# A hybrid encoder layer: the second FFN matrix loaded once, kept on chip and mixed in place, with another order of the products

## The chip, the cores and the metric

The kernel runs on one core of a Trainium2 chip. The metric is the device time of the program in microseconds. The profile shows one execution of it. TensorE (PE) multiplies matrices, and its loads of the stationary operand have a row of their own (PEld). VectorE (DVE), ScalarE (ACT) and GpSimd (POOL) work element by element. SyncE (SP) issues transfers (DMA) from its queue, in order.

## The reference, cut to what matters

The layer computes, for 1024 tokens of width 1024: modulated RMS norm, a combined projection, two attention mixers, a gated merge and an output projection with a residual, and then a gated feed-forward network (FFN) with a residual. The change lies in the last line of it, the second FFN matrix of 2816 x 1024:

```python
h2 = rms_norm(x, g_norm2[l]) * (1.0 + sc2) + sh2
a, up = jnp.split(h2 @ w_ffn_in[l], 2, axis=-1)
x = x + gt2 * ((jax.nn.silu(a) * up) @ w_ffn_out[l])
```

## The kernel before, in words

**Precision.** Every operand of a large product is split in two, a high half `whi` (a copy by ACT, line 118) and a low half `wlo` (a subtraction on DVE or POOL, line 119). A block product is then three matmuls: high x high, high x low, low x high (`PASS`). `wload` fetches a block of 128 x 512 into one of six small `raw` tiles on the SP queue. `wsplit` makes its halves in ten `whi` and ten `wlo` tiles. As a step takes two of each, at most five steps of the inner loop are on chip as halves at a time.

**The second FFN matrix.** The gated activations (1024 x 2816) and the matrix (2816 x 1024) are cut into 2 x 2 blocks, and their product is formed with seven block products instead of eight (Strassen's scheme in Winograd's form). The combinations of the activations were formed in the stage before and lie in DRAM as `ga_d[g, k]`, transposed, seven of them with eleven tiles of 128 x 512 each. The matrix enters the first three products as plain blocks B11, B21, B22, and the last four as differences:

- T1 = B12 - B11, T3 = B22 - B12, T2 = B22 - T1, T4 = B21 - T2.

`PRODS` gives for each product the combination of the activations and the block of the matrix. In the order of the kernel before the products are P1, P2, P3, P6, P5, P7, P4. `prod2(n)` forms one of them: for each of the eleven steps k it calls `operands` (load and split both sides) and then issues 12 matmuls into four PSUM banks, 132 in all. The last product issues its last three steps together, bank by bank (`LASTK`). Consecutive products use two sets of four banks in turn.

**Where the matrix comes from.** In the first three products `operands` loads a plain block through a raw tile (`wload(w2blk(...))`). Besides, during the second and third products, `w2_mix(k)` loads all four blocks of row k again into 44 resident tiles of the pool `w2m` (88 KB per partition), and forms the four differences in place on DVE (lines 1477 to 1480). The last four products read them from there. Low halves of the resident tiles are made by POOL for k < 10 in the fourth to sixth product and k < 5 in the seventh, all others by DVE.

**Memory.** The pool `f2`, which holds `gt2`, the outputs `c11` to `c22` and the `x2` tiles, takes the place of `h2T`, the operand of the first FFN matrix. `gt2` is the first tile in it and lies where the first half of `h2T` lay, so its load (line 1465) waits for the last matmul that reads it. The pool `w2m` takes the place of the pools of the first FFN matrix, from the end where `t3` and `t2` lay, which the last column product no longer reads.

**The outputs.** After each product DVE adds its banks into the blocks `c11`, `c12`, `c21`, `c22` that need it (ACT copies the first). `finish` then scales a finished block by `gt2` (DVE, line 1522), adds the residual `x2` loaded from DRAM (POOL, line 1523) and stores it. The last block, `c21`, is scaled and gets its residual ahead of the last product. P4 is then scaled and added bank by bank (lines 1557, 1558) and stored.

**What sets the order.** TensorE's order is the written one throughout (`manual_schedule`). In this last stage the order on ACT, DVE, POOL and SP is set by the framework's planner, which places instructions in the order in which they become ready in its own simulated time. `pin` (`keep_in_program_order`) ties an instruction behind the one that was written just before it for the same engine. It is an order of issue and not a wait for completion. The loads of the resident tiles are pinned.

Of the kernel before, what the change touches and what calls it, by code (L numbers as in the profile page):

```python
# [10 lines left out]
F32 = mybir.dt.float32  # L11
# [9 lines left out]
HT = 11  # L21
# [22 lines left out]
def hybrid_layer(ctx: ExitStack, tc: tile.TileContext, x, colp, wada1, wada2, bada2, wqkv, wg, wpa, wpb,  # L44
                 wo, w1, w2, hgain, ropeg, rope, rbias, bmask, g2r, out):
    nc = tc.nc

    def pool(name, side, **kw):
        return tc.alloc_tile_pool(name=name, bufs=1, side=side, reuse_waits="tile", **kw)
# [25 lines left out]
    def bank(tag):  # L75
        return ps.tile([128, 512], F32, tag=tag, name="ps_" + tag)
# [29 lines left out]
    def fview(ap):  # L106
        return ap.bitcast(F32)

    def wload(src, n):
        raw = wp.tile([128, 512], F32, tag="raw", bufs=NRAW, name="raw")  # L110
        nc.sync.dma_start(raw[:, :n], src)
        return raw[:, :n]

    def wsplit(r, eng=None):
        n = r.shape[1]
        hi = wp.tile([128, 512], F32R, tag="hi", bufs=NHL, name="whi")
        lo = wp.tile([128, 512], F32R, tag="lo", bufs=NHL, name="wlo")
        nc.scalar.activation(hi[:, :n], r, AF.Copy)  # L118
        (eng or nc.gpsimd).tensor_sub(lo[:, :n], r, fview(hi[:, :n]))  # L119
        return hi, lo  # L120
# [404 lines left out]
    class Cluster:  # L525
# [5 lines left out]
        def add(self, I):  # L531
            I.c0 = self.keys
            self.items.append(I)
            self.keys += I.nkb * 128
# [204 lines left out]
    pin = tc.keep_in_program_order  # L739
# [726 lines left out]
    def w2blk(r, c, k):  # L1466
        return w2[(k + HT * r) * 128:(k + HT * r + 1) * 128, c * 512:c * 512 + 512]

    w2p = pool("w2m", "right")
    w2m = {}  # L1470

    def w2_mix(k):
        b = [w2p.tile([128, 512], F32, name=f"m{n}_{k}") for n in range(4)]
        for z, (r, c) in zip(b, ((0, 0), (0, 1), (1, 1), (1, 0))):
            pin(nc.sync.dma_start(z, w2blk(r, c, k)))
        t1, t3, t2, t4 = b
        nc.vector.tensor_sub(t1, t3, t1)  # L1477
        nc.vector.tensor_sub(t3, t2, t3)  # L1478
        nc.vector.tensor_sub(t2, t2, t1)  # L1479
        nc.vector.tensor_sub(t4, t4, t2)  # L1480
        w2m[k] = t1, t2, t3, t4

    PRODS = ((0, (0, 0)), (1, (1, 0)), (6, (1, 1)), (4, 1), (3, 0), (5, 2), (2, 3))
    LASTK = 3

    def operands(n, k):
        g, m = PRODS[n]
        a = wload(ga_d[g, k], 512)
        b = w2m[k][m] if n > 2 else wload(w2blk(*m, k), 512)
        return wsplit(a, nc.vector), wsplit(b, nc.vector if n < 3 or k == HT - 1 or (n == 6 and k > 4) else None)  # L1490

    def blocks(name):
        return [fp.tile([128, 512], F32, name=f"{name}{m}") for m in range(4)]

    def prod2(n):
        pb = [bank(("ds", "vt")[n % 2][m // 2]) for m in range(4)]
        last = LASTK if n == 6 else 0

        def mm(k, m, o):
            for i, (a, b) in enumerate(PASS):  # L1500
                nc.tensor.matmul(pb[m], o[0][a][:, m * 128:(m + 1) * 128], o[1][b],  # L1501
                                 start=(k == 0 and i == 0), stop=(k == HT - 1 and i == 2))

        for k in range(HT - last):
            o = operands(n, k)
            if n in (1, 2) and k % 2 == n - 1:
                w2_mix((k + (n - 1) * HT) // 2)
            for m in range(4):
                mm(k, m, o)
        ops = {k: operands(n, k) for k in range(HT - last, HT)}  # L1510
        for m in range(4):
            for k in ops:
                mm(k, m, ops[k])
        return pb

    def finish(rh, c, z, last=None):
        cs = slice(c * 512, c * 512 + 512)
        for m in range(4):
            t = rh * 4 + m
            xt = fp.tile([128, 512], F32, tag="x2", bufs=4, name="x2")  # L1520
            nc.sync.dma_start(xt, x2_d[t * 128:(t + 1) * 128, cs])
            nc.vector.tensor_mul(z[m], z[m], gt2[:, cs])  # L1522
            nc.gpsimd.tensor_add(z[m], z[m], xt)
            if last is None:
                nc.sync.dma_start(out[t * 128:(t + 1) * 128, cs], z[m])

    c11, c12, c21, c22 = (blocks(z) for z in ("c11", "c12", "c21", "c22"))
    add = nc.vector.tensor_add
    p1 = prod2(0)
    for m in range(4):  # L1530
        nc.scalar.activation(c21[m], p1[m], AF.Copy)
    p2 = prod2(1)
    for m in range(4):
        add(c11[m], c21[m], p2[m])  # L1534
    p3 = prod2(2)
    for m in range(4):
        add(c12[m], c21[m], p3[m])
    p6 = prod2(3)
    for m in range(4):
        add(c21[m], c21[m], p6[m])  # L1540
        add(c12[m], c12[m], p6[m])
    finish(0, 0, c11)
    p5 = prod2(4)
    for m in range(4):
        add(c22[m], c21[m], p5[m])
        add(c12[m], c12[m], p5[m])
    finish(0, 1, c12)
    p7 = prod2(5)
    for m in range(4):
        add(c21[m], c21[m], p7[m])  # L1550
        add(c22[m], c22[m], p7[m])
    finish(1, 1, c22)
    finish(1, 0, c21, True)
    p4 = prod2(6)
# [111 lines left out]
```

## Time and profile before

| | |
|---|---|
| median of the runs | 1508.73 us (1504.3 to 1509.01, three runs) |
| profiled execution, its own time | 1513.95 us |
| its span, first to last instruction | 1512.1 us, 24226 instructions |
| mean granted TensorE clock | 0.998 |
| last stage (line 1501), starts of the first and last matmul | 1295.3 and 1507.1 us |
| second FFN matrix, resident tiles | 44 loads of 256 KB (line 1475) |

All durations in the prediction are of the profiled execution; its own time stands above the median of the runs. In a timeline a row has the start, the duration, the engine with its line and operation, the tile written and the tiles read, and in brackets the idle time before it and what ended it. The duration of a DVE instruction overlaps that of the next a little, so the pitch between two starts is the smaller number. `SPq` rows are issues of transfers, not their landing.

### The profile page before, as it was taken

The page shows a single profiled execution, that of the slowest core. Times are in us where ns is not written, and L with a number is a line of the kernel's source. Part 1 is how long each engine was busy: PE and PEld are TensorE (multiplying, and loading weights), DVE is VectorE, ACT ScalarE, POOL GpSimd, SP SyncE. Part 2 cuts the span into 40 slices and gives each one's busy share as a digit, 9 for nine tenths or more (in the row PEclk, how much of TensorE's full clock was granted, in tenths as well). Part 3 has the DMA queues.
Part 4 walks back from the last instruction along what each step waited for, and adds up shares of the span by engine and source line. Part 5 has one row for each costly group of instructions (what it writes and reads, how often), then busy time and mean ns, then how long its engine had stood idle before and what let it go on. Part 6 is the DMA issues. An engine that isn't in the chain of part 4 may idle for free. (4 is left out here: it accounts for less than half of the span.)

```text
span 1512.1 us, 24226 instructions
## 1 busy us (share of the span) xinstructions
PE 1488.8 (98%) x8156; PEld 1267.5 (84%) x8156; DVE 1063.0 (70%) x2201; ACT 697.0 (46%) x1755; POOL 537.0 (36%) x540
## 2 busy tenths in 40 slices
PE   8999999999999999999999999999999999999998
PEld 7998989998888877788878888888888888887886
DVE  6877777766778724366565497788867777599468
ACT  5555665565766665245532344332222333354442
POOL 0332332321100040002361311677777776104464
PEclk9999999999999999999999999999999999999999
DMA  9625455645145164823553235345443334798342
GB/s 353 247 75 172 140 159 162 196 137 166 53 134 167 48 194 142 325 87 115 175 172 148 82 102 181 115 137 174 154 138 106 105 106 146 263 384 281 100 151 101
DMA packets 150636, 241.64 MB, mean 160 GB/s; under 512 B 26464, under 2 KB 69088, under 8 KB 149744
## 3 DMA queue, kind: packets, MB, share of 16 engines
q1 hardware_dynamic: 131936, 226.45, 45.6%
q10 hardware_dynamic: 18576, 13.64, 2.8%
q8 instruction: 65, 1.06, 0.3%
q14 instruction: 59, 0.48, 0.1%
HBM read 179.89 MB, written 60.15 MB: 159 GB/s over the span
## 5 line engine op out<-in xcount | busy, mean ns | idle before, releaser
L119 POOL TENSOR_TENSOR wlo<-raw,whi 128x512 fp32r<-128x512 f32 (+2 forms) x133 | 175.3, 1331 | 462.9 <-ACT whi L118 395.5
L118 ACT ACTIVATE whi<-raw 128x512 fp32r<-128x512 f32 (+1 forms) x348 | 203.1, 598 | 250.9 <-PE ps_t L1501 35.4
L312 PE MATMUL ps_d<-whi,hT 128*128 128x384 f32 x1152 | 311.1, 341 | 0.0
L119 DVE TENSOR_TENSOR wlo<-raw,whi 128x512 fp32r<-128x512 f32 (+1 forms) x215 | 184.3, 870 | 81.2 <-ACT whi L118 76.3
L312 PEld LDWEIGHTS ps_d<-whi,hT 128*128 128x128 f32 x1152 | 210.3, 189 | 5.2 <-ACT vs L350 2.6
L312 PE MATMUL ps_d<-wlo,hT 128*128 128x384 f32 x576 | 193.8, 336 | 1.8 <-DVE wlo L119 1.7
L312 PEld LDWEIGHTS ps_d<-wlo,hT 128*128 128x128 f32 x576 | 108.9, 189 | 2.8 <-DVE wlo L119 2.3
L118 ACT ACTIVATE whi<-ws 128x512 fp32r<-128x512 f32 x65 | 40.8, 628 | 127.3 <-DVE ws L1348 86.3
L1281 POOL TENSOR_TENSOR e<-e,c 128x512 f32<-128x512 f32 x44 | 69.0, 1569 | 60.5 <-DVE c L1411 36.4
L342 POOL TENSOR_TENSOR ra<-qn,rtab 128x64 f32<-128x64 f32 x48 | 16.3, 339 | 156.0 <-DVE qn L335 106.1
L119 POOL TENSOR_TENSOR wlo<-m,whi 128x512 fp32r<-128x512 f32 x35 | 51.4, 1478 | 54.7 <-ACT whi L118 54.7
L1279 ACT ACTIVATE e<-e 128x512 f32<-128x512 f32 x44 | 27.5, 630 | 91.4 <-DVE e L1414 64.0
L555 ACT ACTIVATE P<-P,st 128x256 f32<-128x256 f32 (+2 forms) x100 | 45.7, 458 | 39.7 <-DVE st L553 39.6
L712 PE MATMUL ps_d<-hT,whi 128*128 128x512 f32 x192 | 60.6, 397 | 0.0
L1331 PE MATMUL ps_v<-h2T,whi 128*128 128x512 f32 x192 | 59.2, 390 | 0.0
L1331 PE MATMUL ps_s<-h2T,whi 128*128 128x512 f32 x192 | 59.1, 389 | 0.0
L1331 PE MATMUL ps_d<-h2T,whi 128*128 128x512 f32 x184 | 56.8, 390 | 0.0
L129 ACT ACTIVATE ry<-ss,eps 128x4 f32<-128x4 f32 (+1 forms) x88 | 26.2, 298 | 64.7 <-DVE ss L333 47.8
L119 DVE TENSOR_TENSOR wlo<-ws,whi 128x512 fp32r<-128x512 f32 x45 | 49.7, 1106 | 8.5 <-ACT whi L118 8.5
L1280 DVE TENSOR_TENSOR e<-e 128x512 f32<-128x512 f32 x44 | 42.6, 975 | 16.6 <-ACT e L1279 16.5
L301 DVE SCALAR_TENSOR_TENSOR acc<-wa,cact,acc 128x512 f32<-128x512 f32 x56 | 42.0, 749 | 16.7 <-DMA wa<-in_wada_dram 16.5
L491 ACT ACTIVATE P<-P,sx 128x384 f32<-128x384 f32 (+1 forms) x64 | 37.1, 580 | 35.9 <-DVE sx L490 35.9
(445 smaller groups left out, 3965.6 us busy)
## 6 DMA issues: line engine op xcount, KB each, us to landing
raw<-in_w_dram SPq DMA_DIRECT2D x139, 256.0 KB
ga_d<-e SPq DMA_DIRECT2D x77, 256.0 KB
raw<-ga_d SPq DMA_DIRECT2D x77, 256.0 KB
wa<-in_wada_dram SPq DMA_DIRECT2D x32, 512.0 KB
raw<-in_wqkv_dram SPq DMA_DIRECT2D x80, 192.0 KB
m<-in_w_dram SPq DMA_DIRECT2D x44, 256.0 KB
raw<-in_wg_dram SPq DMA_DIRECT2D x42, 256.0 KB
xt<-in_x_dram SPq DMA_DIRECT2D x16, 512.0 KB
```

Of the source, the lines that this page charges most:

```text
L118: nc.scalar.activation(hi[:, :n], r, AF.Copy)
L119: (eng or nc.gpsimd).tensor_sub(lo[:, :n], r, fview(hi[:, :n]))
L129: nc.scalar.activation(y, ss, AF.Ln, scale=1.0 / n, bias=eps)
L301: nc.vector.scalar_tensor_tensor(ada_acc[c], wa, cact[:, kk:kk + 1], ada_acc[c], op0=ALU.mult, op1=ALU.add)
L312: nc.tensor.matmul(pd[:, :384], tok(a, k, t), U.w[k][b][:, :384], start=(k == 0 and i == 0), stop=(k == KT - 1 and i == 2))
L491: nc.scalar.activation(P[:nq, :nk], P[:nq, :nk], AF.Exp, scale=-1.0, bias=nm, accum_out=sm)
L555: nc.scalar.activation(C.P[h][:nq, c], C.P[h][:nq, c], AF.Exp, scale=-1.0, bias=nm, accum_out=sm)
L712: nc.tensor.matmul(st["p"], gw[i, br][j][a][:, kk * 128:(kk + 1) * 128], hT[b][:, k, hs], start=(k == 0 and q == 0), stop=(k == 7 and q == 2))
L1279: nc.scalar.activation(sg, a, AF.Sigmoid)
L1280: nc.vector.tensor_mul(sg, sg, a)
L1281: nc.gpsimd.tensor_mul(sg, sg, up)
L1331: nc.tensor.matmul(pb, w[p][:, k * 128:(k + 1) * 128], b[q][:, k], start=(k == 0 and i == 0), stop=(k == 3 and i == 2))
```

## The change

The resident tiles are loaded once and serve all seven products. `w2_load(s)` is called three steps ahead (`LOOK`). It loads the block that the product reads: B11 in the first, B21 together with B12 in the second, and B22 in the third, 44 loads in all, each pinned. The first three are written ahead of the first product, right behind the load of `gt2`. `operands` takes the matrix from these tiles in every product, so only the activations still go through the raw tiles.

`w2_mix(n, k)` forms one difference per step, in place: T1 in the third product, T3 in the fourth, T2 in the fifth, T4 in the sixth. Each is read one product later. For this the products run as P1, P2, P3, P5, P7, P6, P4. P6 is now added into three outputs after the sixth product, which makes four additions more, and `c12` is finished there, together with `c22` and `c21`, and no longer after the fifth. Low halves of the matrix are now made by DVE, except for k < 5 of the seventh product, which stay on POOL.

```diff
--- before.py
+++ after.py
@@ -1467,27 +1467,34 @@
         return w2[(k + HT * r) * 128:(k + HT * r + 1) * 128, c * 512:c * 512 + 512]
 
     w2p = pool("w2m", "right")
-    w2m = {}
-
-    def w2_mix(k):
-        b = [w2p.tile([128, 512], F32, name=f"m{n}_{k}") for n in range(4)]
-        for z, (r, c) in zip(b, ((0, 0), (0, 1), (1, 1), (1, 0))):
-            pin(nc.sync.dma_start(z, w2blk(r, c, k)))
-        t1, t3, t2, t4 = b
-        nc.vector.tensor_sub(t1, t3, t1)
-        nc.vector.tensor_sub(t3, t2, t3)
-        nc.vector.tensor_sub(t2, t2, t1)
-        nc.vector.tensor_sub(t4, t4, t2)
-        w2m[k] = t1, t2, t3, t4
-
-    PRODS = ((0, (0, 0)), (1, (1, 0)), (6, (1, 1)), (4, 1), (3, 0), (5, 2), (2, 3))
-    LASTK = 3
+    w2t = {}
+    PRODS = ((0, (0, 0)), (1, (1, 0)), (6, (1, 1)), (3, (0, 0)), (5, (0, 1)), (4, (1, 1)), (2, (1, 0)))
+    LASTK, LOOK = 3, 3
+
+    def w2_load(s):
+
+        n, k = divmod(s, HT)
+        if n < 3:
+            for b in (PRODS[n][1],) + (((0, 1),) if n == 1 else ()):
+                w2t[b, k] = w2p.tile([128, 512], F32, name=f"m{b[0]}{b[1]}_{k}")
+                pin(nc.sync.dma_start(w2t[b, k], w2blk(*b, k)))
+
+    def w2_mix(n, k):
+
+        t1, t3, t2, t4 = (w2t.get((b, k)) for b in ((0, 0), (0, 1), (1, 1), (1, 0)))
+        if n == 2:
+            nc.vector.tensor_sub(t1, t3, t1)
+        elif n == 3:
+            nc.vector.tensor_sub(t3, t2, t3)
+        elif n == 4:
+            nc.vector.tensor_sub(t2, t2, t1)
+        elif n == 5:
+            nc.vector.tensor_sub(t4, t4, t2)
 
     def operands(n, k):
-        g, m = PRODS[n]
+        g, b = PRODS[n]
         a = wload(ga_d[g, k], 512)
-        b = w2m[k][m] if n > 2 else wload(w2blk(*m, k), 512)
-        return wsplit(a, nc.vector), wsplit(b, nc.vector if n < 3 or k == HT - 1 or (n == 6 and k > 4) else None)
+        return wsplit(a, nc.vector), wsplit(w2t[b, k], None if n == 6 and k < 5 else nc.vector)
 
     def blocks(name):
         return [fp.tile([128, 512], F32, name=f"{name}{m}") for m in range(4)]
@@ -1502,9 +1509,9 @@
                                  start=(k == 0 and i == 0), stop=(k == HT - 1 and i == 2))
 
         for k in range(HT - last):
+            w2_load(n * HT + k + LOOK)
             o = operands(n, k)
-            if n in (1, 2) and k % 2 == n - 1:
-                w2_mix((k + (n - 1) * HT) // 2)
+            w2_mix(n, k)
             for m in range(4):
                 mm(k, m, o)
         ops = {k: operands(n, k) for k in range(HT - last, HT)}
@@ -1526,6 +1533,8 @@
 
     c11, c12, c21, c22 = (blocks(z) for z in ("c11", "c12", "c21", "c22"))
     add = nc.vector.tensor_add
+    for k in range(LOOK):
+        w2_load(k)
     p1 = prod2(0)
     for m in range(4):
         nc.scalar.activation(c21[m], p1[m], AF.Copy)
@@ -1535,20 +1544,21 @@
     p3 = prod2(2)
     for m in range(4):
         add(c12[m], c21[m], p3[m])
-    p6 = prod2(3)
-    for m in range(4):
-        add(c21[m], c21[m], p6[m])
-        add(c12[m], c12[m], p6[m])
     finish(0, 0, c11)
-    p5 = prod2(4)
+    p5 = prod2(3)
     for m in range(4):
         add(c22[m], c21[m], p5[m])
         add(c12[m], c12[m], p5[m])
-    finish(0, 1, c12)
-    p7 = prod2(5)
+    p7 = prod2(4)
     for m in range(4):
         add(c21[m], c21[m], p7[m])
         add(c22[m], c22[m], p7[m])
+    p6 = prod2(5)
+    for m in range(4):
+        add(c12[m], c12[m], p6[m])
+        add(c22[m], c22[m], p6[m])
+        add(c21[m], c21[m], p6[m])
+    finish(0, 1, c12)
     finish(1, 1, c22)
     finish(1, 0, c21, True)
     p4 = prod2(6)
```

## The prediction

> **What bounds the kernel now.** I read the page's busy shares first, then the last stage (the second FFN matrix, seven products of 132 matmuls) cut into its seven products, and then the timelines of the engines at the places where the change acts. The columns of the second fence are the stretch and its length, and then busy time and instructions of PE, PEld, DVE, ACT and POOL, the granted clock, the DMA share and GB/s.
>
> ```profile
> PE 1488.8 (98%) x8156; PEld 1267.5 (84%) x8156; DVE 1063.0 (70%) x2201; ACT 697.0 (46%) x1755; POOL 537.0 (36%) x540
> ```
>
> ```profile
> 1295.30:1325.20 29.90, 29.90 (x133) 24.79 (x132) 18.18 (x27) 12.26 (x21) 5.56 (x4) 1.00 0.96 325
> 1325.20:1355.20 30.00, 30.00 (x134) 24.83 (x134) 29.10 (x48) 16.44 (x28) 0.00 (x0) 1.00 1.04 385
> 1355.20:1387.00 31.80, 31.15 (x134) 24.52 (x133) 30.81 (x44) 12.22 (x21) 8.67 (x6) 1.00 0.98 341
> 1387.00:1417.00 30.00, 30.00 (x134) 24.87 (x133) 16.21 (x20) 13.48 (x25) 19.00 (x13) 1.00 0.45 122
> 1417.00:1446.90 29.90, 29.90 (x134) 24.77 (x133) 13.91 (x21) 12.68 (x23) 13.20 (x10) 1.00 0.32 99
> 1446.90:1476.80 29.90, 29.90 (x134) 24.76 (x133) 23.82 (x25) 12.68 (x23) 21.47 (x14) 1.00 0.51 168
> 1476.80:1507.70 30.90, 30.49 (x133) 24.26 (x131) 28.09 (x34) 7.94 (x14) 14.35 (x9) 1.00 0.29 100
> ```
>
> TensorE sets the time. A product costs it 29.9 us when nothing is late, which is 11 steps k of 2.72 us. Only the third (31.8, so 1.9 lost, of which I count 1.8 because its ends are rounded) and the seventh (30.9, 1.0 lost) are longer. So this stage has 2.8 us to give, and no edit in it can gain more than that. Every new wait of TensorE, however, is paid in full. The third product is the one where DVE (30.81 of 31.80) and the DMA engines (0.98) are both full. In the seventh DVE is full until the last operands are split:
>
> ```profile
> 1480.00:1490.00 10.00, 10.00 (x12) 1.00 0.48 161
> 1490.00:1500.00 10.00, 10.00 (x11) 1.00 0.20 75
> ```
>
> ```profile
> 1500.02 0.40 PE L1501 MATMUL ps_d<-whi 128*128 128x512 f32 x1
> 1500.66 0.51 PE L1501 MATMUL ps_d<-wlo,whi 128*128 128x512 f32 x1 [0.24 <-DVE wlo L119]
> ```
>
> Here TensorE stands for the last low half. DVE has no slack left in the seventh product, and this decides most of what follows.
>
> **The start of the stage.** In the kernel before, the blocks of the second matrix for the first three products go through the small raw tiles and were fetched during the first FFN matrix. In the changed kernel they go to the resident tiles, and each of these loads is pinned, that is, it stands on the SP queue behind the SP instruction that was written just before it. For the very first one that is the load of `gt2` (line 1465). The pin holds in the kernel before: the first resident load there left SP directly behind the raw load that is written ahead of it.
>
> ```profile
> 1312.24 0.36 SPq L111 DMA_DIRECT2D raw<-in_w_dram  x1
> 1312.64 1.47 SPq L1475 DMA_DIRECT2D m<-in_w_dram  x2
> ```
>
> `gt2` lies where the first half of `h2T` lay, so its load waits for the last matmul of the first FFN matrix, the one at 1295.09:
>
> ```profile
> 1295.09 0.39 PE L1331 MATMUL ps_v<-h2T,wlo 128*128 128x512 f32 x1
> 1295.32 0.39 PE L1501 MATMUL ps_d<-whi 128*128 128x512 f32 x1
> ```
>
> ```profile
> 1295.26 0.66 SPq L1285 DMA_DIRECT2D ga_d<-e  x1
> 1296.27 0.32 SPq L1465 DMA_DIRECT2D gt<-mod_d  x1
> 1296.65 0.91 SPq L1521 DMA_DIRECT2D x<-x_d  x2
> 1297.67 0.37 SPq L111 DMA_DIRECT2D raw<-in_w_dram  x1
> 1298.08 0.92 SPq L1521 DMA_DIRECT2D x<-x_d  x2
> ```
>
> TensorE begins the stage at 1295.32. The first block of the matrix can now leave SP no earlier than 1296.65, behind `gt2` (512 KB), and perhaps behind some of the four `x2` loads that become ready with it. Behind the pinned loads queue the others of the first product, and TensorE's order is fixed, so it has nothing else to do. What a load takes from issue to first use on an otherwise idle queue is seen at the kernel's start, where eight tiles of 512 KB are fetched:
>
> ```profile
> 1.65 3.87 SPq L171 DMA_DIRECT2D xt<-in_x_dram  x8
> ...
> 4.96 1.06 ACT L203 ACTIVATE hT<-xt 128x1024 fp32r<-128x1024 f32 x1 [2.18 <-DMA xt<-in_x_dram]
> ...
> 6.36 1.23 DVE L205 CUSTOM_DVE_ANT_0 hT<-xt 128x1024 fp32r<-128x1024 f32 x1 [2.71 <-DMA xt<-in_x_dram]
> ```
>
> The first 512 KB are used 3.31 us after issue and the next 1.40 later, so 256 KB behind another transfer add 0.70. `gt2` then lands at 1296.27 + 3.31 = 1299.58 and the first block at 1300.28. ACT makes its high half and DVE its low half:
>
> ```profile
> L118 ACT ACTIVATE whi<-raw x34: 614/632/651, 1262.1 to 1328.6; 128x512 fp32r<-128x512 f32 x34
> L119 DVE TENSOR_TENSOR wlo<-raw,whi x32: 679/686/1774, 1263.8 to 1329.5; 128x512 fp32r<-128x512 f32 x32
> ```
>
> The first matmul starts at 1300.28 + 0.63 = 1300.91, which is 5.6 us late. The second one needs the low half 0.69 after the high one instead of 0.23 after its predecessor, another 0.4. That makes 6.0. One `x2` load ahead adds 0.7, and all four add 2.8. The smallest value is a block that lands alone (3.31 - 0.70 = 2.6 after 1296.65, and SP some 0.7 earlier than here), 4.3. I take **6.7** out of 4.3 to 8.8, with one `x2` load ahead, since in the rows above two went ahead of the load that was next. The later blocks follow at 0.7 us against 2.72 of matmuls, so they cost nothing more.
>
> **Products one to three.** Removed are 33 loads of 256 KB, since 77 loads of the matrix become 44. The DMA share of 0.96 to 1.04 falls by 33 of some 110 loads. In the third product DVE keeps 22 splits and has 11 differences. If DMA and DVE both leave TensorE alone there, the 1.8 us come back: **-1.8**. The planner may start differences earlier than written (their data are there), which would keep DVE as full as now, so the bounds are -1.8 and +2.
>
> **Products four to six.** 30 low halves move from POOL to DVE, and so do 33 differences in the third to fifth, and the sixth product. A difference in a chain takes 0.73 from one to the next, a split 0.60:
>
> ```profile
> 1336.37 0.69 DVE L1479 TENSOR_TENSOR m<-m,m 128x512 f32<-128x512 f32 x1
> 1337.10 0.69 DVE L1480 TENSOR_TENSOR m<-m,m 128x512 f32<-128x512 f32 x1
> ...
> 1498.12 0.68 DVE L119 TENSOR_TENSOR wlo<-raw,whi 128x512 fp32r<-128x512 f32 x1
> ```
>
> A product then asks DVE for 22 x 0.60 + 11 x 0.73 + 8 additions x 0.60 = 26.0 of 29.9 us. The cover is the ten split slots, of which eight are four steps (10.9 us) ahead of TensorE, against a burst of 8 x 0.60 = 4.8 at each product's end. I cost it at **0**. Without the cover each burst would cost up to 4.8.
>
> **The seventh product.** Here the new order of products shows. P6 now comes sixth and is added into three outputs, so 12 additions follow instead of 8, and `c12` is scaled and finished together with `c22` and `c21`, 12 scalings on DVE and 12 additions of `x2` on POOL instead of 8 and 8. The stretch before:
>
> ```profile
> 1475.27 0.68 DVE L1550 TENSOR_TENSOR c<-c,ps_v 128x512 f32<-128x512 f32 x1
> 1475.86 0.68 DVE L1551 TENSOR_TENSOR c<-c,ps_v 128x512 f32<-128x512 f32 x1
> ...
> 1490.71 1.78 DVE L119 TENSOR_TENSOR wlo<-m,whi 128x512 fp32r<-128x512 f32 x1
> ...
> 1499.92 0.68 DVE L119 TENSOR_TENSOR wlo<-m,whi 128x512 fp32r<-128x512 f32 x1
> ```
>
> ```profile
> 1490.27 6.77 POOL L1523 TENSOR_TENSOR c<-c,x 128x512 f32<-128x512 f32 x4 [1.23 <-DVE c L1522]
> ```
>
> From 1475.27 to 1500.60 DVE runs 29 instructions without a pause (16 additions and scalings, 13 splits) in 25.3 us. At 0.60 each that would be 17.4; the other 7.9 fall on the eight POOL additions, 1.0 each, and one split beside POOL does take 1.78 instead of 0.68. Eight more on DVE and four more on POOL are 8 x 0.60 + 4 x 1.0 = **+8.8**, ahead of the last split, because the planner takes instructions as they become ready. All of it reaches TensorE, which already stands for that split. The upper bound is all eight at 1.78, 14.2. The lower is 0, if they come behind the last split, where DVE has 5.9 us free:
>
> ```profile
> 1500.00:1512.00 12.00, 7.29 (x31) 5.37 (x29) 6.14 (x9) 0.00 (x0) 0.00 (x0) 0.99 0.23 89
> ```
>
> The tail (last matmuls, scaling, store) is unchanged.
>
> **Sum.** 6.7 - 1.8 + 0 + 8.8 = +13.7 us on the profiled execution's own 1513.95 (span 1512.1), so 1527.6. That execution is 5.2 above the median of the runs (1508.73), so for the median I say **1522.4**.
>
> **The rivals.**
> The first is that the long wait at the start also slows the matmuls behind it. The trace has a slow beginning: after the start TensorE runs 21 of its 128-wide matmuls in 4 us, and later 12 in one, all at a clock shown as granted in full.
>
> ```profile
> 2.00:6.00 4.00, 4.00 (x21) 4.00 (x20) 0.93 (x7) 1.26 (x4) 0.00 (x0) 1.00 0.83 286
> 7.00:8.00 1.00, 1.00 (x12) 1.00 (x11) 0.76 (x3) 0.30 (x1) 0.00 (x0) 1.00 1.04 410
> ```
>
> ```profile
> PE ps_d L1266 <- DVE sg L1128: 2.1, 1, 2.1
> ```
>
> If the wait of 6 us brings that state back for as long, 21 matmuls take 4 us instead of 1.8: +2.2, so 1524.6. Against it, the longest wait inside the kernel is 2.1 us, and says nothing of 6. [...]
>
> The second ends on the other side, not slower by what can be told. It is the planner's order in the seventh product: the eight added instructions stand behind the last split. The price there is then 0 and the sum 6.7 - 1.8 = +4.9, 1513.6, and with the start at its low bound +2.5, 1511.2. It decides from the point where more than seven of the eight go behind. Against it, the eight scalings of before all stand ahead of the last ten splits.
>
> The third is that the first blocks are on chip in time after all (issued before some 1291), because the pin doesn't hold them behind `gt2`. Then -1.8 + 8.8 = +7.0, 1515.7. The two rows at 1312 speak against it.
>
> The fourth is that the differences are started as early as their data allow and crowd the third product. 22 of them more there are 16.1 us of DVE beside a product in which it has 30.81 of 31.80 taken; less the 10.9 of cover, +5.2 on the sum, 1527.6.
>
> **How the numbers follow.** Forecast 0.53, clock 0.17, behind the last split 0.14, start covered 0.06, third product crowded 0.10. 0.3% of the median (4.5 us) is about what a measurement of this kernel can tell from no change. Half of the second rival, 0.07, lies within it, and I add 0.03 for it joined with the third. Joined in full they would give at most the 2.8 us of lost time, which is no gain that can be told; for a surprise I leave 0.03. So faster 0.03, same 0.10, slower 0.87. The range runs from 1510 (start at its low bound, seventh product nearly free) to 1531 (start at 8.8 and crowded or slow matmuls).
>
> **What would show it.** Right: the first load of a resident tile leaves SP right behind that of `gt2`, TensorE has one gap of 5 to 8 us ahead of the first product, the third product takes 30 us, products four to six 29.9 with POOL nearly idle, and the seventh some 39 with DVE full and TensorE waiting for low halves. Wrong: a first product without a gap, or a seventh of at most 32 us. A slow row of matmuls behind the gap would speak for the clock.

## The result and the profile after

The changed kernel takes 1532.43 us (median of four runs, 1529.85 to 1535.21), the kernel before in the same session 1508.87 us. The ratio is **1.0163, with an interval of 1.0132 to 1.0193**: 23.6 us slower. The prediction said slower, with 13.7 us as its sum; the time lies 1.4 us above its range.

The profiled execution after took 1529.85 us (span 1528.1). These are the seven products of the last stage, preceded by the gap ahead of them, in the stretches view of the kernel after. Columns: the stretch and its length; busy time and instructions of PE, PEld, DVE, ACT and POOL; granted clock; DMA share; GB/s.

```profile
1283.65:1301.60 17.95, 0.00 (x0) 0.00 (x0) 2.07 (x4) 1.29 (x3) 5.04 (x4) 0.55 0.66 225
1301.60:1333.90 32.30, 32.28 (x133) 26.27 (x133) 25.15 (x40) 17.18 (x31) 0.00 (x0) 0.93 0.99 367
1333.90:1363.80 29.90, 29.90 (x133) 24.78 (x132) 24.84 (x40) 13.19 (x25) 0.00 (x0) 1.00 0.54 175
1363.80:1393.70 29.90, 29.90 (x133) 24.77 (x132) 29.90 (x44) 12.69 (x22) 6.35 (x4) 1.00 0.48 155
1393.70:1423.60 29.90, 29.90 (x133) 24.76 (x133) 18.77 (x31) 12.70 (x22) 0.00 (x0) 1.00 0.37 111
1423.60:1453.50 29.90, 29.90 (x133) 24.75 (x133) 18.72 (x31) 12.69 (x22) 0.00 (x0) 1.00 0.31 96
1453.50:1483.50 30.00, 30.00 (x135) 24.82 (x133) 17.02 (x28) 12.72 (x23) 5.16 (x4) 1.00 0.34 99
1483.50:1523.50 40.00, 32.82 (x133) 25.49 (x131) 37.19 (x42) 8.05 (x14) 21.04 (x13) 0.91 0.40 129
```

Set beside the rows of before, four places differ: a gap of 18.0 us in which TensorE does nothing, a first product 2.4 us longer (32.3 against 29.9), a third 1.9 shorter, and a seventh 9.1 longer (40.0 against 30.9). Their sum is 18.0 + 2.4 - 1.9 + 9.1 = +27.6. The stage as a whole, from the last matmul of the first FFN matrix to the end, grew from 1512.1 - 1295.1 = 217.0 to 1528.1 - 1283.3 = 244.8, which is +27.8 (1283.26 is the start of that last matmul after). The work ahead of it is the same in the same order, and yet it ended 11.8 us earlier in the one profiled execution than in the other; in the profiles below it ends between 1281.1 and 1288.2. So a comparison of whole spans of two single profiles is up to 14 us uncertain here, and the stage is compared by itself.

**The gap.** The timelines of the kernel after, in the order of the chain (the row has start, duration, engine, line and operation; in brackets the idle time before and what ended it):

```profile
1283.26 0.39 PE L1331 MATMUL ps_v<-h2T,wlo 128*128 128x512 f32 x1
1283.68 0.32 SPq L1465 DMA_DIRECT2D gt<-mod_d  x1
...
1291.93 1.26 POOL L1288 TENSOR_TENSOR e<-e 128x512 f32<-128x512 f32 x1 [4.78 <-DMA ga_d<-e]
...
1293.22 3.72 SPq L1293 DMA_DIRECT2D ga_d<-e  x4
1294.61 1.26 POOL L1290 TENSOR_TENSOR e<-e 128x512 f32<-128x512 f32 x1
1295.90 0.69 DVE L1291 TENSOR_TENSOR e<-e 128x512 f32<-128x512 f32 x1 [10.09 <-POOL e L1290]
1297.28 5.82 SPq L1480 DMA_DIRECT2D m<-in_w_dram  x11
1300.93 0.63 ACT L118 ACTIVATE whi<-m 128x512 fp32r<-128x512 f32 x1 [15.84 <-DMA m<-in_w_dram]
1301.62 0.79 PE L1508 MATMUL ps_d<-whi 128*128 128x512 f32 x1 [17.97 <-ACT whi L118]
```

The first resident load does not leave SP behind `gt2` at 1283.68, but 13.6 us later, behind the last of the four stores of line 1293. These store the last combinations of activations from the tiles `e` of the first FFN stage, which POOL and DVE form only after TensorE is done. In the view of SP's waits those in between stand at these stores and at one of line 1285 ahead of them, 8.9 us together, and none at the load itself: it has its place in the queue behind them. The load then needs 3.65 us until ACT has it.

**The seventh product.** The same view of its last part:

```profile
1482.03 0.68 DVE L1558 TENSOR_TENSOR c<-c,ps_v 128x512 f32<-128x512 f32 x1
...
1503.50 10.07 POOL L1530 TENSOR_TENSOR c<-c,x 128x512 f32<-128x512 f32 x6 [1.23 <-DVE c L1529]
...
1512.35 1.77 DVE L119 TENSOR_TENSOR wlo<-m,whi 128x512 fp32r<-128x512 f32 x1
...
1515.85 0.68 DVE L119 TENSOR_TENSOR wlo<-m,whi 128x512 fp32r<-128x512 f32 x1
```

From the first addition to the end of the last split DVE takes 1516.53 - 1482.03 = 34.5 us; before it was 25.3. Beside POOL's run of residual additions a split takes 1.77, after it 0.68.

### The profile page after: what moved, and what is told of

Its sections match the earlier page's. It is cut to its first block, busy times and chain, and to the rows that moved or that the text cites. A ratio compares the mean times of both kernels' runs of the same rounds, so it can differ in the third digit from the quotient of the medians.

```text
span 1528.1 us, 24083 instructions
## 1 busy us (share of the span) xinstructions
PE 1487.3 (97%) x8156; PEld 1267.0 (83%) x8156; DVE 1073.7 (70%) x2235; ACT 695.1 (45%) x1755; POOL 490.1 (32%) x510
## 5 line engine op out<-in xcount | busy, mean ns | idle before, releaser
L118 ACT ACTIVATE whi<-raw 128x512 fp32r<-128x512 f32 (+2 forms) x315 | 183.5, 595 | 233.0 <-PE ps_s L1508 59.5
L119 DVE TENSOR_TENSOR wlo<-raw,whi 128x512 fp32r<-128x512 f32 (+1 forms) x182 | 148.2, 815 | 84.5 <-ACT whi L118 82.8
L119 DVE TENSOR_TENSOR wlo<-m,whi 128x512 fp32r<-128x512 f32 x72 | 52.3, 727 | 5.0 <-ACT whi L118 5.0
L118 ACT ACTIVATE whi<-m 128x512 fp32r<-128x512 f32 x77 | 47.4, 616 | 15.8 <-DMA m<-in_w_dram 15.8
```

## The experiments

Two readings of the gap stood against each other: the pin behind `gt2` (the prediction's), or the pool of the resident tiles. Two terms had to be separated in the first product (clock or late blocks) and two in the seventh (the number of DVE instructions or POOL's additions). Last, what a kernel without both losses is worth.

### The first product's blocks in a pool of their own

```diff
     w2p = pool("w2m", "right")
+    w2q = pool("w2f", "right")
...
+                if n == 0:
+                    w2t[b, k] = w2q.tile([128, 512], F32, name=f"m00_{k}")
```

The 33 other tiles are made at once in `w2m`. The eleven of B11 keep their place: the programs built from the two kernels have them at the same addresses, where `t3` and part of `t2` lay. What changes is the pool that they belong to. The pins stay.

> The changed kernel, but the eleven tiles of block B11 (first product) lie in a pool of their own, where t3 and part of t2 lay; the other 33 resident tiles stay where t1, the c tiles and the e tiles lay. Theory A (the long gap ahead of the last stage comes from the pool: the whole pool w2m is held, in the planned order of SP, behind the last use of the e tiles, the four ga_d stores of line 1293): the loads of B11 leave SP before the end of the first FFN matrix, the gap of 18.0 us falls to 1 us or less, the slow matmuls behind it (2.4 us) go too, and the time falls by 19 to 20, to about 1513. Theory B (the prediction's: the pin holds the first load behind that of gt2): a gap of 6 us and more stays, and the time is 1518 to 1522.

Measured: 1519.93 us against 1506.69 of the kernel before on the same chip, ratio 1.0093 (1.0064 to 1.0122). Products 30.6, 29.9, 29.9, 34.8, 29.9, 29.9, 39.9. SP's timeline at the start of the stage:

```profile
1285.37 2.23 SPq L1482 DMA_DIRECT2D m<-in_w_dram  x5
1287.70 0.38 SPq L1285 DMA_DIRECT2D ga_d<-e  x1
1288.17 0.38 SPq L1465 DMA_DIRECT2D gt<-mod_d  x1
1288.60 3.55 SPq L1482 DMA_DIRECT2D m<-in_w_dram  x4
```

Five resident loads now leave ahead of `gt2` although the pins are there, and the first product starts at 1288.89 with no wait beyond 1 us. So the gap came from the pool: in one pool with the other 33, whose memory also covers that of `e`, the eleven were held back until the last reader of `e` was done, although they lie over none of that memory. The 33 are held here too: the first of them leaves SP at 1310.98, behind the last store of line 1293. The time alone, 1519.9, would fit the other theory; it is theory A's with a new loss of 4.9 us, in the fourth product, that neither had foreseen. It is followed up below.

### The pins taken off

```diff
-                pin(nc.sync.dma_start(w2t[b, k], w2blk(*b, k)))
+                nc.sync.dma_start(w2t[b, k], w2blk(*b, k))
```

> The changed kernel without the pin on the loads of the resident tiles. Theory A (the pool): the gap stays at about 18 us and the time at about 1532. Theory B (the pin behind gt2): the first load leaves SP as soon as its tile is free, the gap is 0 to 2 us and the time about 1513.

Measured: 1531.79 us, a single run. SP's timeline:

```profile
1284.40 0.32 SPq L1465 DMA_DIRECT2D gt<-mod_d  x1
...
1294.38 3.73 SPq L1293 DMA_DIRECT2D ga_d<-e  x4
1298.44 4.79 SPq L1480 DMA_DIRECT2D m<-in_w_dram  x10
```

The same gap, 18.5 us, without any pin. With the run before, this settles it: the pin had no part in the gap. Why a pin written right behind the load of `gt2` lets loads pass ahead of it was not looked into; what is said of the pin ahead of the prediction does not hold for these loads.

### The old order of products and outputs

Products again P1, P2, P3, P6, P5, P7, P4, with `c12` finished after the fifth product and P6 added into two blocks after the fourth. T1 is formed in the second product, T3 and T2 in the third, T4 in the fourth. Loads as in the change.

```diff
-    PRODS = (..., (3, (0, 0)), (5, (0, 1)), (4, (1, 1)), (2, (1, 0)))
+    PRODS = (..., (4, (1, 1)), (3, (0, 0)), (5, (0, 1)), (2, (1, 0)))
```

> The changed kernel, single loads and one pool, but with the products and the outputs in the order of the kernel before (P6 fourth); the differences are formed as T1 in the second product, T3 and T2 in the third, T4 in the fourth. Theory A (the seventh product is long because 8 more DVE and 4 more POOL instructions stand ahead of the last split): the seventh product falls from 40.0 to about 31 us and its slow matmuls go; the gap of 18 us stays; the time is about 1523 to 1524, with up to 2 us more if DVE is overfull in the third product. Rival (the seventh product is long because the low halves of the matrix moved to DVE, not because of the order): it stays at 38 or more and the time at about 1532.

Measured: 1524.09 us (1523.38 to 1531.9), ratio 1.0124 (1.0096 to 1.0152). The gap, the first and the seventh product in its stretches view:

```profile
1286.40:1303.95 17.55, 0.00 (x0) 0.00 (x0) 2.08 (x4) 1.31 (x3) 5.05 (x4) 0.59 0.65 220
1303.95:1336.92 32.97, 32.97 (x133) 26.82 (x133) 25.32 (x40) 17.27 (x31) 0.00 (x0) 0.91 0.99 363
1486.52:1517.30 30.78, 30.53 (x133) 24.38 (x131) 28.00 (x33) 8.05 (x14) 14.83 (x9) 1.00 0.31 102
```

The seventh product is back at 30.8 with the pool, the single loads, the pins and the division of the low halves as in the change. So the order of the products costs the 9 us, and the low halves that moved from POOL to DVE cost nothing.

### Both together, without pins

```diff
+    w2q = pool("w2f", "right")
...
-    PRODS = (..., (3, (0, 0)), (5, (0, 1)), (4, (1, 1)), (2, (1, 0)))
+    PRODS = (..., (4, (1, 1)), (3, (0, 0)), (5, (0, 1)), (2, (1, 0)))
...
-                pin(nc.sync.dma_start(w2t[b, k], w2blk(*b, k)))
+                nc.sync.dma_start(w2t[b, k], w2blk(*b, k))
```

> Both together, without the pin: B11 in its own pool and the order of the products of the kernel before. If the two causes add: 1532 - 19.5 - 9 = about 1504, which is 5 us below the kernel before; products one to six at 29.9, the seventh at about 31. If the crowded third product or the DMA takes it back: 1508 or more.

Measured: 1509.10 us (1507.51 to 1517.19, ten runs), ratio 1.0023 (1.0007 to 1.0038). The gap falls to 1.2 us and the seventh product is repaired, but products are 30.6, 29.9, 30.6, 32.9, 29.9, 29.9, 30.8: the loss in the fourth is here too. Its timelines, and the additions of line 1531 taken singly (count; shortest, median and longest in ns; first and last start):

```profile
1353.77 20.41 POOL L1531 TENSOR_TENSOR c<-c,x 128x512 f32<-128x512 f32 x4 [47.76 <-issue]
...
1368.58 0.71 DVE L1493 TENSOR_TENSOR m<-m,m 128x512 f32<-128x512 f32 x1
...
1374.45 0.44 SPq L1533 DMA_DIRECT2D out_dram<-c  x1
...
1376.38 8.50 SPq L111 DMA_DIRECT2D raw<-ga_d  x7
1377.09 0.69 DVE L119 TENSOR_TENSOR wlo<-raw,whi 128x512 fp32r<-128x512 f32 x1 [7.80 <-ACT whi L118]
```

```profile
L1531 POOL TENSOR_TENSOR c<-c,x x4: 1288/1288/16674, 1353.8 to 1372.9; 128x512 f32<-128x512 f32 x4
```

The four residual additions of `c11` take 20.4 us on POOL, where the same four took 6.35 in the kernel after. It is the first that is held, by its record for 16.7 us; the other three take 1.29 each. Beside the first, DVE starts an instruction every 0.60 us without a pause, the last at 1368.58, and the addition ends 1.1 us after that one, at 1370.4. The stores of `c11` wait for POOL, and the loads of the fourth product's activations stand behind them on SP's queue, so DVE then waits 7.8 us.

### TensorE kept busy through the gap

```diff
+    pw = bank("t")
+    for i in range(150):
+        nc.tensor.transpose(pw[:, :128], ident, ident)
     p1 = prod2(0)
```

> The changed kernel with 150 transposes of the identity written between the last product of the first FFN stage and the first product of this one; they fill TensorE's 18 us wait and add nothing to the output. Theory A (the 2.4 us by which the first product was longer than the others come from the clock after the wait): the first product takes 29.9 to 30.5 us instead of 32.3, its matmuls follow each other at 0.227 us from the first one, and the wait for the first resident block, seen as the start of the first product, stays where it was. Theory B (the 2.4 us come from blocks that arrive late): the first product still takes 32.3 us. Both: seventh product near 40 us, fourth to sixth 29.9.

Measured: 1526.08 us, a single run. TensorE's timeline and the first product in the stretches view:

```profile
1281.29 16.54 PE L1540 MATMUL ps_t<-ident 128*128 128x128 f32 x150
1299.52 0.51 PE L1508 MATMUL ps_d<-whi 128*128 128x512 f32 x1 [1.70 <-ACT whi L118]
```

```profile
1299.52:1330.08 30.56, 30.34 (x132) 24.89 (x133) 24.44 (x39) 17.16 (x31) 0.00 (x0) 1.00 1.03 384
```

The wait itself stays: from the end of the last matmul to the first is 18.1 us. The first product, however, falls from 32.3 to 30.6, and its granted clock reads 1.00 instead of 0.93. So 1.7 of the 2.4 us were slow matmuls behind the idle time. The rest, 0.6, is also there in the runs in which B11 has a pool of its own. It lies in the first two matmuls, which are followed by the next after 0.73 and 0.34 us instead of 0.23, as TensorE waits there for the first low half. That is theory A, just outside its range of 29.9 to 30.5. In the three other profiles with the gap and without the transposes the first product takes 32.5 to 33.0, so the slow matmuls cost 1.7 to 2.4.

### Three quarters of the output without residual

```diff
-            nc.gpsimd.tensor_add(z[m], z[m], xt)
+            if (rh, c) == (0, 0):
+                nc.gpsimd.tensor_add(z[m], z[m], xt)
```

> The changed kernel without the residual in three of the four quarters of the output: the loads of x2 and the twelve additions on GpSimd in the finishes of c12, c22 and c21 are left out; the twelve VectorE additions of the sixth product's result and the twelve gate products stay. Theory A (the seventh product's 9.2 us are VectorE's eight more instructions at 0.60 us, 4.8 us, and GpSimd's additions that stretch VectorE's by about 1.0 us each): without the twelve additions VectorE's stretch falls by about 12 us, from 34.5 to about 22 to 23 us, its last split comes before TensorE needs it, and the seventh product takes 30 to 31 us. Theory B (the eight instructions behind one another on VectorE set it, whatever GpSimd does): the stretch falls by little and the seventh product stays at 36 us or more. Both: the wait of 18 us and the slow first product stay.

The twelve loads of `x2` for these additions are left out too. Measured: 1525.12 us, a single run. The seventh product in its stretches view, and the first addition and last split on DVE:

```profile
1488.96:1519.05 30.09, 30.09 (x133) 24.59 (x131) 25.24 (x41) 8.06 (x14) 1.29 (x1) 1.00 0.28 104
```

```profile
1487.49 0.68 DVE L1560 TENSOR_TENSOR c<-c,ps_v 128x512 f32<-128x512 f32 x1
...
1509.37 0.68 DVE L119 TENSOR_TENSOR wlo<-m,whi 128x512 fp32r<-128x512 f32 x1
```

With the same DVE instructions and without POOL's twelve additions the stretch is 1510.05 - 1487.49 = 22.6 us instead of 34.5. The difference is 11.9, so 1.0 per addition, and 22.6 is 37 instructions at 0.61. The seventh product then takes 30.1 us, as theory A has it.

### Plain raw tiles for the first product

From the run with the old order, with one pool and no pins: B11 is fetched through the raw tiles in the first product, as before, and all 44 resident loads follow, 55 loads instead of 77.

```diff
+            for b in ((), ((1, 0), (0, 1), (0, 0)), ((1, 1),))[n]:
...
-        return wsplit(a, nc.vector), wsplit(w2t[b, k], None if n == 6 and k < 5 else nc.vector)
+        return wsplit(a, nc.vector), wsplit(w2t[b, k] if n else wload(w2blk(*b, k), 512), ...)
```

> The order of products of the kernel before; the first product's eleven blocks come through the raw tiles as there, and only behind them are all 44 quarter blocks loaded to stay: 55 loads instead of 77. Theory A (the resident tiles' place behind the pool of the first FFN stage costs only the blocks that are wanted at the start; products 2 and 3 draw their blocks early enough): no wait ahead of the first product, products of 29.9 to 30.6 us, the third 1.2 to 1.9 us shorter than before's 31.8, seventh 30.9: 0 to 2 us under the kernel before. Theory B (GpSimd's residual additions of c11 are starved when VectorE runs on without waiting, and the stores and loads queue behind them): the fourth product loses 3 to 5 us as in the two runs with a pool of their own, and the kernel is 1 to 3 us slower than before.

Measured: 1506.32 us against 1506.63, ratio 1.0000 (0.9985 to 1.0015). No gap; products 29.9, 30.6, 32.6, 29.9, 29.9, 29.9, 30.8. Theory A held for the start and the first two products, but the third is longer than before's 31.8 and not shorter; theory B did not hold, as the fourth lost nothing. In its stretches view DVE is full there, with POOL's four additions at their ordinary 1.6 us beside it:

```profile
1346.48:1379.11 32.63, 31.04 (x134) 24.47 (x132) 32.63 (x48) 13.17 (x25) 6.31 (x4) 1.00 0.52 161
```

### The residual of `c11` on DVE

The run with both repairs, and one edit:

```diff
-            nc.gpsimd.tensor_add(z[m], z[m], xt)
+            (nc.vector if (rh, c) == (0, 0) else nc.gpsimd).tensor_add(z[m], z[m], xt)
```

> The kernel with the old order of products and the first product's blocks in a pool of their own (products 30.6, 29.9, 30.6, 32.9, 29.9, 29.9, 30.8), with one edit: the four residual additions of c11 go from GpSimd to VectorE. Theory A (the fourth product's 3.0 us come from those additions, of 5 us each on GpSimd beside a VectorE that is busy without a pause, which hold up the four stores of c11 and behind them on SyncE's queue the loads of the fourth product's blocks): the additions take 0.7 us each, the fourth product takes 29.9 to 30.6 us, and the kernel is 2 to 3 us shorter than without the edit, level with the kernel before or up to 1 us under it. Theory B (the loads are late for another reason, such as the transfers of the resident blocks): the fourth product stays at 32 us or more.

Measured: 1505.27 us against 1506.63, ratio 0.9990 (0.9979 to 1.0001). Products 30.6, 29.9, 29.9, 29.9, 29.9, 29.9, 30.8. The third and fourth product in its stretches view:

```profile
1349.97:1379.88 29.91, 29.91 (x133) 24.78 (x132) 29.91 (x50) 12.69 (x23) 0.00 (x0) 1.00 0.50 161
1379.88:1409.81 29.93, 29.93 (x134) 24.78 (x133) 19.63 (x33) 12.70 (x23) 0.00 (x0) 1.00 0.34 108
```

The fourth product is whole again: the held additions and the queue behind them were its loss. (The 5 us each of the expectation are the mean of one of 16.7 and three of 1.29.) The seven products take 211.0 us, the least of all, against 212.2 before. But TensorE waits 1.1 us ahead of the first, and from the start of the last matmul of the first FFN matrix to the end of the last of all both kernels take 212.4 us. So the stage is level with before, and the interval of the ratio touches 1.

### The same edit in two other kernels

> The kernel with the old order, the first product's blocks through the raw tiles and 55 loads (products 29.9, 30.6, 32.6, 29.9, 29.9, 29.9, 30.8), with the one edit that took 3 us off the other variant: c11's four residual additions go from GpSimd to VectorE. In that kernel VectorE's six slowed instructions beside them took about 1.1 us more each in the third product. Theory A (the third product's 2.7 us come from GpSimd's four additions beside a full VectorE): the six are back at 0.68 us, less 6 x 1.1 = 6.6 us against 4 x 0.6 = 2.4 us more, so the third product falls to 29.9 or 30.6 us and the kernel is 2 us shorter, 1503 to 1505. Theory B (VectorE has too many instructions in the third product: two differences per row, two splits per row): it stays at 32 us or more.

Measured, in the variant with raw tiles for the first product: 1505.51 us against 1507.04, ratio 0.9992 (0.9982 to 1.0002). The third product in the stretches view falls from 32.6 only to 31.4:

```profile
1314.45:1345.18 30.73, 30.43 (x133) 24.62 (x132) 23.31 (x38) 13.23 (x26) 0.00 (x0) 1.00 0.99 376
1345.18:1376.54 31.36, 30.50 (x134) 24.62 (x132) 31.36 (x53) 13.24 (x25) 0.00 (x0) 1.00 0.53 169
```

> The kernel before with that same edit alone: c11's four residual additions go from GpSimd to VectorE; all 77 loads stay. Theory A (the third product's 31.8 us there come from the same additions, not from the 33 blocks that are loaded twice): the third product falls to 29.9 to 30.6 us and the kernel is 1.2 to 1.9 us shorter than before, so that single loading is worth nothing measurable. Theory B (the third product is long because of the transfers or the crowd of differences): it stays at 31.8 us and the time stays the same.

Measured, in the kernel before: 1506.35 us, ratio 0.9996 (0.9984 to 1.0007). Its third product is no shorter, 32.8 instead of 31.8:

```profile
1346.77:1379.61 32.84, 30.81 (x133) 24.62 (x132) 30.98 (x51) 13.65 (x24) 2.20 (x2) 1.00 0.98 343
```

In both, theory A was wrong or only half right: there POOL's additions are not all that makes the third product long. In the first, 53 DVE instructions fill it without POOL (31.36 of 31.36 busy), while in the second product, with the DMA engines at 0.99, DVE had 38 and time to spare. (Beside POOL's additions four DVE instructions were slowed in the run without this edit, to 1.45, 1.78, 1.78 and 1.77 us, and not the six that the expectation counts.) That late blocks push DVE's work from the second product towards the third is likely but not shown: the differences formed in the third are 17 here and 17 in the run above with the residual of `c11` on DVE, where it takes 29.9. In the kernel before with this edit DVE is nearly full and the DMA engines are at 0.98. The run above had 50 DVE instructions in its third product, with the DMA engines at 0.50, and lost nothing. So the number of DVE instructions alone does not make before's third product long, and the transfers are likely; no run changes them alone.

## Why the prediction was wrong

**The start of the stage (+6.7 predicted, +18.6 measured: the gap of 18.0 and 0.6 for the low half behind it).** This is the step that failed, and the cause it gave is wrong, not only the size. It said that the pin puts the first resident load right behind `gt2`, and read that off two neighbouring rows at 1312. Without pins the gap is 18.5 us, and with the tiles in their own pool loads pass `gt2` in spite of the pins. What holds the load is its pool: all 44 tiles wait for the last use of the tiles `e` in the stage before, whose memory the pool covers in part. The trace of before had a row that would have raised the question, three rows ahead of the first of the two, in SP's timeline:

```profile
1310.63 0.38 SPq L1293 DMA_DIRECT2D ga_d<-e  x1
...
1312.64 1.47 SPq L1475 DMA_DIRECT2D m<-in_w_dram  x2
```

There too the first resident load leaves only once the last store of `e` has gone; nobody waited for it then. By itself this pair proves as little as the one that was quoted, but it recurs in every profile here, with pins and without, for the first load into `w2m`. The chain that the sum should have followed is the one shown above: 1283.65 to 1297.28 until the stores are out, 13.6 us, then 3.65 for the load and 0.7 for the first half, 18.0 together. The prediction had the block landed 1300.28 - 1296.65 = 3.63 us after its own issue, and 3.65 were measured. That is luck in part: its 3.63 held a wait behind the transfer of `gt2`, which had long been done here, and for a block alone it had 2.6.

**Slow matmuls behind the gap (a rival, priced +2.2; measured +1.7, which goes when TensorE is kept busy).** It happened, beside the forecast and not in place of it. The other 0.6 of the first product's 2.4 is the low half, for which the prediction had 0.4. The first matmuls behind the gap follow each other at 0.43 us instead of 0.23. TensorE's timeline after the 6.6 us wait in the seventh product of the kernel after shows the same, and the return:

```profile
1507.41 0.80 PE L1508 MATMUL ps_d<-wlo,whi 128*128 128x512 f32 x1 [6.59 <-DVE wlo L119]
1508.01 0.63 PE L1508 MATMUL ps_d<-whi,wlo 128*128 128x512 f32 x1
1508.43 0.63 PE L1508 MATMUL ps_d<-whi 128*128 128x512 f32 x1
...
1510.96 0.40 PE L1508 MATMUL ps_s<-whi 128*128 128x512 f32 x1
```

Here it is at full pace again after 3.5 us; the slow row behind the gap lasts 4.6 us, from 1301.62 to 1306.24. The trace of before has the same behind the longest wait inside it, in TensorE's timeline:

```profile
781.20 3.88 PE L1266 MATMUL ps_d<-wr,h2T 128*128 128x512 f32 x9 [2.13 <-DVE sg L1128]
784.92 0.41 PE L1266 MATMUL ps_d<-whi,h2T 128*128 128x512 f32 x1
```

These nine follow each other at 0.41 us, and the granted clock is 0.54 from 781.20 to 784.92 and 1.00 from there to 788. So the wait of 2.1 us, of which the prediction held that it "says nothing of 6", spoke for this rival. A single long wait is not needed: in the run with a pool of its own for B11, two waits of 1.7 and 0.9 us with one matmul between them were followed by matmuls at 0.43 us too. The nine intervals from 1385.33 to 1389.09 take 3.76 us instead of 2.04 at 0.227 each, which makes some 1.7 of the 4.9 us that its fourth product lost, at a granted clock of 0.95 over that product. The wait of 1.7 us in the run with TensorE kept busy, with one of 0.2 behind it, was followed by full pace from the third matmul on. What a wait must be like to bring the slow row is not shown. In the seventh product the slow row costs nothing: from the end of the last split to the end of the last matmul are 6.9 us in both kernels.

**Products one to three (-1.8; measured -1.9): right in size, and partly by luck.** The third takes 29.9 us, with DVE just full. But what fills it is not what was said. The planner did not leave the differences where they were written, but formed all 44 in the first three products, T2 and T4 too, as the groups by line of the third product show (the group, busy time, mean ns of one, idle time before):

```profile
L1490 DVE TENSOR_TENSOR m<-m,m 128x512 f32<-128x512 f32 x8 | 5.4, 678 | 0.0
L1492 DVE TENSOR_TENSOR m<-m,m 128x512 f32<-128x512 f32 x8 | 6.5, 815 | 0.0
```

These are 16 in a product for which 11 were written. That is the fourth rival's mechanism. It had 22 more in mind and priced them at +5.2; five more cost nothing, as DVE is full there (29.90 of 29.90) but not late. In the kernel before, the third product held 16 differences too, so the relief of DVE that the term counted on did not come. What fell is the share of the DMA engines, from 0.98 to 0.48.

**Products four to six (0): right,** 29.9 each, and with more room than was worked out: DVE has 17 to 19 us instead of 26.0, because no difference is left for them.

**The seventh product (+8.8; measured +9.1): right,** by its own working: 34.5 us of DVE against 34.1 predicted, eight instructions at 0.60 and four POOL additions at 1.0, all ahead of the last split. The run without residual separates the two terms, the run with the old order gives the whole back. The second rival (behind the last split) did not occur. The third rival (start covered) was right that the pin doesn't hold, and wrong that the blocks are then in time.

The sum with the measured gap and slow matmuls, 18.0 + 2.4 - 1.9 + 9.1, accounts for the stage's 27.8 within 0.2. The medians differ by 23.6; that some 4 us less are seen in them is within what the unchanged stages ahead vary from one profile to the next, and was not followed further.

## What to carry to other kernels

When a transfer into on-chip memory moves earlier, ask what the memory under its whole pool still holds and who is the last to read or store that, and look for the pair "last store, first load" in the queue of the kernel before; neighbours in a queue are no proof of what ties them. Price the two repairs before the change: here a pool of their own for the eleven urgent tiles removed 17 us of waiting, and not moving the output work into the last product 9 us. The single loading itself was worth nothing that shows: no variant has a shorter stage than the 212.4 us of before, and the best stands at 0.9990 (0.9979 to 1.0001).

## What the runs showed of the hardware that was not expected

DVE and POOL hinder each other in two ways. In the seventh product of the kernel after, POOL's additions keep 1.64 to 1.74 us, and a DVE split, with both operands in SBUF, that they hold up takes 1.74 to 1.78 instead of 0.68; additions from PSUM stay at 0.67 to 0.68, beside POOL instructions of 1.3. In the third product of the kernel with the old order, POOL's four additions take 1.60 on average, and the ten splits of the activations 0.87. In the two kernels in which B11 has a pool of its own and POOL makes the additions, DVE keeps its pace of 0.60, and one POOL addition takes 16.7 us, until DVE's unbroken run is over; the three behind it take 1.29 each. In the other of the two the four take 22.9 together, so that the first has some 19.1 if the others take as long there. So one of the two engines is kept out, in the second case through 25 and 29 DVE instructions in a row. What decides which of the two engines loses stays open.

The first way cost 1.0 us of DVE per addition, 11.9 in the seventh product. In the second DVE kept its pace, and yet it reached TensorE, because SP's queue carried it on: late stores held up loads that TensorE needed, at 3.0 and 4.9 us.
